# Hybrid attention block: other slots for the sums of x, part of them reloaded in the last unit, larger transfers, and two column blocks of w_out split early and kept in DRAM

## The chip, the core and the metric

The kernel runs on one core of a Trainium2 chip. The metric is device time in microseconds (us) of one execution; the median of several runs counts. A core has TensorE (PE; PEld is its weight load), VectorE (DVE), ScalarE (ACT), GpSimd (POOL) and SyncE (SP, which here issues nearly all DMAs). Each engine works through its own queue in order.

## The reference

The block takes x (2048 tokens by 1024), normalizes it, projects it with w_in, runs two attention mixers (A: a window of 128; B: three dilated groups), gates each with a SiLU path, projects each branch, merges both with sigmoid gates and adds a last projection to x:

```python
h = rms_norm(x, norm_gain[layer])
proj = h @ w_in[layer]
qa, ka, va, qb, kb, vb, ga, gb, mg = jnp.split(proj, split_idx, axis=-1)
...
br_a = ya @ w_branch_a[layer]
br_b = yb @ w_branch_b[layer]
gates = jax.nn.sigmoid(mg.reshape(bsz, S, N_BRANCHES, D).astype(jnp.float32)
                       + b_merge[layer].astype(jnp.float32)).astype(x.dtype)
merged = gates[:, :, 0] * br_a + gates[:, :, 1] * br_b
x = x + merged @ w_out[layer]
```

## The kernel before

Every large product is made of fp16 pairs: a float32 operand is scaled by a power of two and split into a high and a low half (ACT writes the high half, DVE the low one), and three matmuls (high-high, high-low, low-high) stand for one.

**Order of work.** All instructions are written out by hand in time order. `at(t, f)` puts a step on a heap, and `until(t)` emits what is due between the matmuls. In the main stage t counts pairs of projections, in the tail it counts microseconds that the schedule assumes. The constants at the head (T_..., X_...) are these times. A time only sets the place in each engine's queue; what an engine then does depends on what it waits for.

**Pair loop.** There are 14 units of 8 pairs (one unit: a group of heads of A or B). In a pair TensorE projects two blocks of 128 tokens (L735) into the banks `pj`; ACT and DVE take out q, k and v (v's low half at L767), normalize, and SP turns q and k into `kq` by a DMA transpose (L820). Two or three pairs later come the logits (L905), DVE's bias and maximum (L920), ACT's exponentials, a transpose of the probabilities (`pt`, L943) and the products with v (L954). In the third unit of each head pair the three groups of B are merged (L1118 to L1144, then `YPart`).

**Sums of x.** The gate stage uses a Strassen-like scheme of 7 products instead of 8, in which one factor is a block sum of the normalized x: S1 to S4, with two halves p of 512 tokens and 4 chunks c each. `x_sums` (L1223) makes them inside the pair loop, on DVE and ACT, in the tile `sx` (slots 0 to 3 are float32 scratch, 4 to 6 the two halves of a result), and SP stores them to DRAM (`xsd`). The 128 steps are spread evenly over the stretches of pairs in X_SUM.

**Gate stage.** After pair 111 come 12 merge-gate and gate projections, then six groups of 14 products (`gate_group`, L1563; each product has 12 matmuls). `xs_load` (L1490) first brings the sums back: S2 into the tiles `Y00` and `Y01` of pool `y0`, S3 and S1 into slots 2 and 3 of `wt` (with leftovers in `sx` slots 4 to 6), S4 into a free part of XH and XL. T_X holds their times. The products use S2, S3, S1 and S4 in that order in the first group. Beside this `prep` brings each next group's weights: SP loads them (`w_load`, L195), POOL multiplies by the gains (L200), ACT squares (L247), a small matmul sums over partitions (L219), DVE makes the scale, ACT and DVE split (L272, L282); `w_sums` (L1530, L1533) makes the sums of the weights. The small matmul stands in TensorE's queue at a fixed place.

**w_out.** Its four column blocks j are loaded by `b_load` (L1425, four transfers of 256 KB) and split by `b_blocks` (L1415, L1416: seven blocks with three in-place subtractions and one more at L1437) into slot j of `wt`, which the last stage reads. Before, j = 0, 1 and 2 were split in the gate stage (at 68, 103 and 204), using `sx` slots 0 to 3 as raw tile; j = 3 in the branch stage (66), using the tile `wraw`.

**Branch and output stage.** 32 steps of 5.2 us multiply the branch results Y by the branch weights (L359); DVE multiplies each result by its gate (L1708), POOL adds the two (L1715), and `a_blocks` splits the merged blocks (`mm`, L1415 and L1416) and stores them (`mtd`, L1661). PSUM has 8 banks for these results, so TensorE can be at most 8 results ahead of DVE. SP loads the gates three steps ahead (L1698), and near the end of the stage the first merged groups (`M<-mtd`, L1692). The output stage then runs 8 groups of 7 products with `wt` (L1774).

Of the kernel before, what the change touches and what calls it, by code (L numbers as in the profile page):

```python
# [100 lines left out]
X_END = (68.1, 71.1, 75.1)  # L101
X_TH = 1.2
X_SC = (0.25, 0.25, 0.25, 0.0625)
X_SUM = ((5, 16), (19, 33), (44, 59), (68, 83), (93, 104)), 0.2
T_Y = (2.0, 0.8, 1.6, 1.5, 4.0, 26.0, 0.5, 1.3, 2.1, 1.6, 2.0)
T_P = ((0, 0.0, 0.03), (1, 7.0, 31.0), (2, 37.5, 60.5), (3, 69.4, 92.4), (4, 105.8, 128.8), (5, 142.2, 165.2))
T_O = ((0, 60.0, 68.0), (1, 95.0, 103.0), (2, 196.0, 204.0))
T_OB = (58.0, 66.0)
T_G = (173.0, 183.0, 193.0, 194.5)
T_R = (60.0, 1.2)  # L110
T_X = ((1, 0.0), (2, 2.0), (0, 14.0), (3, 22.0))
T_S = (2.0, 11.0, 0.85, 1.6, 0.75, 1.5, 0.9, 1.3, 0.8)
T_H = (176.0, 2.0, 0.02)
T_GATE = (0.1, 0.1, 0.9, 1.0, 1.0)
# [16 lines left out]
def block_kernel(tc, x, w_units, w_gate, w_mrg, w_brn, w_out, w_bra, gain, qkg, sink, bias_a, bias_b, b_merge, out):  # L131
# [54 lines left out]
    def raw_tile():  # L186
        return wp.tile([128, NCH, 384], F32, name="wraw", bufs=1)
# [262 lines left out]
    def at(t, f, *args):  # L450
        seq[0] += 1
        heapq.heappush(heap, (t, seq[0], f, args))
# [796 lines left out]
    def spread(n, parts):  # L1249
# [8 lines left out]
                d -= b - a  # L1258
        return out

    times = spread(128, X_SUM[0])
    for k in range(8):
        x_sums(times[16 * k:16 * k + 16], k // 4, k % 4)
# [2 lines left out]
    t = 0  # L1266
# [102 lines left out]
    def tail_scales():  # L1369

        def tt(*a):
            V.tensor_tensor(*(v[:] for v in a[:-1]), a[-1])

        V.tensor_scalar(so4[:], so[:], 0.25, None, OP.mult)
        for k, (s, inv) in enumerate(((sa, ia), (sb, ib))):
            mi, rm, iv = ucol(), ucol(), ucol()
            for c in range(3):
                tt(mi, mi if c else yi[4 * k], yi[4 * k + c + 1], OP.max)
                yield
            V.reciprocal(rm[:], mi[:])  # L1380
            yield
            tt(rm, rm, s, OP.mult)
            tt(iv, mi, inv, OP.mult)
            yield
            for c in range(4 * k, 4 * k + 4):
                tt(rho[c], rm, yi[c], OP.mult)
            invb.append(iv)
        tt(bnd, invb[0], invb[1], OP.add)
        tt(inv_m, invb[0], invb[1], OP.max)
        yield  # L1390
        V.tensor_scalar(bnd[:], bnd[:], 2.0 ** 31, None, OP.mult)
        V.reciprocal(rmx[:], inv_m[:])
        yield
        s_m, i_m = pow2(bnd[:], "m")
        for c in range(8):
            V.tensor_scalar(rho[c][:], rho[c][:], invb[c // 4][:], rmx[:], OP.mult, OP.mult)
        V.tensor_scalar(inv_m[:], inv_m[:], s_m[:], 0.125, OP.mult, OP.mult)
        V.tensor_scalar(i_o[:], i_m[:], io[:], 16.0, OP.mult, OP.mult)
# [10 lines left out]
    A11, A12, A22, S1, S2, S3, S4 = range(7)  # L1409
    B11, B21, B22, T1, T2, T3, N4 = range(7)  # L1410
    mtd = [dr.tile([4, 128, 7, 4, 2, 128], F16, name=f"mtd{k}") for k in range(2)]
    bw, ms = {}, {}

    def split(hi, lo, v, scale):
# [1 line left out]
                lambda: V.scalar_tensor_tensor(lo, v, scale[:], hi, OP.mult, OP.subtract))  # L1416

    def b_load(j):
        if j < 3:
            rv = sx[:, :4].rearrange("p a b c -> p a (b c)").bitcast(F32)  # L1420
        else:
            rv = raw_tile()[:].rearrange("p a b -> p (a b)")[:, :2048].rearrange("p (a b) -> p a b", b=512)
        for i in range(2):
            for h in range(2):
                nc.sync.dma_start(out=rv[:, 2 * i + h, :], in_=w_out[h, :, 4 * i + j, :])  # L1425
        bw["out", j] = rv

    def b_blocks(t0, j):

        b11, b12, b21, b22 = (bw["out", j][:, k, :] for k in range(4))  # L1430
        sub = {0: (b11, b12, b11), 1: (b12, b22, b12), 3: (b22, b22, b11), 5: (b21, b21, b22)}
        for i, (b, v) in enumerate(((B11, b11), (B22, b22), (B21, b21), (T1, b11), (T3, b12), (T2, b22), (N4, b21))):
            hi, lo = split(wt[0][:, b, j, :], wt[1][:, b, j, :], v, so4)
            at(t0 + T_B[2] * i, hi)
            at(t0 + T_B[2] * i + T_B[3], lambda lo=lo, b=b: (lo(), done.add(("b", j, b))))
            if i in sub:
                at(t0 + T_B[2] * i + T_B[3] + .05, lambda o=sub[i]: V.tensor_tensor(*o, OP.subtract))  # L1437


    def br_load(i):  # L1440
# [39 lines left out]
    def xsum(p, i, c):  # L1480
        m = 4 * p + c
        if i == 1:
            return [s2[p][:, k, c, :] for k in range(2)]
        if i == 3:
            return [X[:, c, 1024 + 512 * p:1536 + 512 * p] for X in (XH, XL)]
        if i == 2 and m > 5 or i == 0 and m > 6:
# [2 lines left out]

    def xs_load(p, i):  # L1490
        assert all(("xs", p, i, c) in done for c in range(4))
        if i == 1:
            for k in range(2):
                nc.sync.dma_start(out=s2[p][:, k], in_=xsd[p][:, i, :, k])
            return
        for c in range(4):
            for k, v in enumerate(xsum(p, i, c)):
                nc.sync.dma_start(out=v, in_=xsd[p][:, i, c, k])

    def xblock(b, c, p):  # L1500
        if b in sidx:
# [101 lines left out]
            yield  # L1603

    t = t0 = clock[0]
    s2 = [y0.tile([128, 2, 4, 512], F16, name=f"Y0{p}") for p in range(2)]
    for i, d in T_X:
        for p in range(2):
            at(t + d + .01 * p, xs_load, p, i)
    at(t + T_R[0], run, tail_scales())  # L1610
    for n, b, d in T_P:
        w_sums(t + d, n)
# [114 lines left out]
    y_part(t + T_Y[4], 2, 6, T_Y[4] - .01, 4)  # L1727
    br_prep(t + T_BR[3], 1)
    br_prep(t + T_BR[4], 2)
    at(t + T_OB[0], b_load, 3)  # L1730
    at(t + T_OB[1], b_blocks, t + T_OB[1], 3)
    y_part(t + T_Y[5], 1, 5)
    left = {}
    for k, (i, q) in enumerate(steps):
# [172 lines left out]
```

## Time and profile before

| | us |
|---|---|
| median of 3 runs | 1914.48 (1914.24 to 1918.62) |
| the profiled execution | 1916.64 |
| its span, first to last instruction | 1914.8 |
| TensorE busy in it | 1887.6 |
| DVE / ACT / POOL busy | 1388.3 / 1157.5 / 760.3 |

The profiler's page gives busy times, groups of instructions by source line, and who waited for whom. The other views used are windows (busy time of each engine between two moments, with the clock that TensorE was granted), waits, the chain that ended last, and timelines; times in them count from the start of the span. In names such as `wt<-xsd` the tile written stands ahead of the arrow. SPq is SP's queue; a row there is the issue of a DMA, not its transfer.

### The profile page before, as it was taken

Reading aid. Unit: us, or ns where it says so; the run is one execution under the profiler, and the core shown is the slowest. Engines: PE = TensorE matmul, PEld = TensorE weight load, DVE = VectorE, ACT = ScalarE, POOL = GpSimd, SP = SyncE. Lnnn points to the kernel's source line nnn. Section 1 sums busy time; section 2 is a strip of 40 time slices with the busy share of each in tenths; the row PEclk is TensorE's granted clock in tenths of the full one; section 3 lists DMA queues with packets and bytes.
Section 4 is the critical chain, followed back from the end, with each engine's and each line's share of the span. In section 5 each row is a group of like instructions: output and inputs, shape, how many; then the busy total and the mean of one; then the engine's idle time right before and its main releaser. Section 6 shows DMA issues by size and latency. Waiting matters only on the chain. (4 is left out here: it accounts for less than half of the span.)

```text
span 1914.8 us, 39519 instructions
## 1 busy us (share of the span) xinstructions
PE 1887.6 (99%) x13493; PEld 1183.4 (62%) x13493; DVE 1388.3 (73%) x3691; ACT 1157.5 (60%) x2692; POOL 760.3 (40%) x1782
## 2 busy tenths in 40 slices
PE   8999999999999999999999999999999999999999
PEld 6566766677766687666876668765434444444444
DVE  7579887898887877878878788777347447876412
ACT  8468776787676776767767677665245444432100
POOL 2224343333456545555545654555011101222543
PEclk9999999999999999999999999999999999999999
DMA  8559988897978878787887878669463345878763
GB/s 290 123 100 177 217 168 166 151 204 167 196 153 180 162 156 168 148 185 159 170 164 143 185 142 163 140 120 197 149 198 105 105 158 182 243 235 258 251 242 146
DMA packets 638601, 333.34 MB, mean 174 GB/s; under 512 B 494272, under 2 KB 572480, under 8 KB 637120
## 3 DMA queue, kind: packets, MB, share of 16 engines
q1 hardware_dynamic: 619968, 322.17, 71.5%
q10 hardware_dynamic: 18432, 8.66, 1.8%
q8 instruction: 105, 1.72, 0.4%
q14 instruction: 96, 0.79, 0.1%
HBM read 138.30 MB, written 73.66 MB: 111 GB/s over the span
## 5 line engine op out<-in xcount | busy, mean ns | idle before, releaser
L735 PE MATMUL pj<-wh,XH 128*128 128x384 f16 x1792 | 585.0, 326 | 4.5 <-DVE vt L767 3.8
L735 PE MATMUL pj<-wh,XL 128*128 128x384 f16 x1792 | 586.8, 327 | 0.0
L735 PE MATMUL pj<-wl,XH 128*128 128x384 f16 x1792 | 585.4, 327 | 0.0
L735 PEld LDWEIGHTS <-XH 128*128 128x128 f16 x3584 | 411.4, 116 | 156.2 <-issue 7.6
L920 DVE CUSTOM_DVE_ANT_0 pr<-s,b,ubuf 128x256 f32<-128x256 f32 (+3 forms) x512 | 218.5, 463 | 44.1 <-PE s L905 42.8
L735 PEld LDWEIGHTS <-XL 128*128 128x128 f16 x1792 | 207.7, 116 | 67.8 <-issue 0.5
L937 DVE SCALAR_TENSOR_TENSOR p<-pr,p 128x512 f16<-128x512 f32 (+2 forms) x256 | 188.4, 736 | 15.2 <-ACT p L933 13.6
L812 POOL COPY spl<-spl 128x256 f16<-128x256 f16 (+1 forms) x224 | 88.6, 425 | 226.3 <-DVE spl L807 223.9
L933 ACT ACTIVATE p<-pr 128x512 f16<-128x512 f32 (+2 forms) x256 | 159.1, 622 | 6.6 <-POOL rs_t L318 0.4
L752 ACT ACTIVATE rw<-pj 128x256 f32<-128x256 f32 (+1 forms) x224 | 86.0, 384 | 109.9 <-PE pj L735 102.6
L905 PE MATMUL s<-kq 128*128 128x256 f16 (+3 forms) x1168 | 147.8, 254 | 3.4 <-DMA kq<-spl 3.4
L954 PEld LDWEIGHTS <-pt 128*128 128x128 f16 x3024 | 125.4, 97 | 33.9
L797 POOL TENSOR_TENSOR rw<-rw,g 128x256 f32<-128x256 f32 (+1 forms) x112 | 89.5, 799 | 124.2 <-DVE rw L791 84.8
L954 PE MATMUL pv<-vt,pt 128*128 128x65 f16 (+1 forms) x3024 | 132.7, 192 | 0.0
L905 PEld LDWEIGHTS <-kq 128*128 128x128 f16 x1184 | 101.6, 98 | 44.9 <-DMA kq<-spl 4.7
L310 POOL TENSOR_TENSOR rs_t<-rs_y 128x8 f32<-128x8 f32 (+1 forms) x112 | 42.0, 375 | 215.7 <-DVE rs_y L302 176.2
L1715 POOL TENSOR_TENSOR kp<-kp,fg 128x512 f32<-128x512 f32 x32 | 45.3, 1419 | 203.5 <-DVE fg L1708 123.1
L791 DVE TENSOR_TENSOR rw<-rw,qr 128x512 f32<-128x512 f32 (+1 forms) x112 | 87.0, 777 | 45.9 <-POOL qr L319 45.3
L928 ACT ACTIVATE pr<-pr,z 128x128 f32<-128x128 f32 (+2 forms) x256 | 98.8, 438 | 35.3 <-DVE z L920 35.1
L359 PE MATMUL fps<-Y,wh 128*128 128x512 f16 x384 | 114.5, 379 | 4.7 <-DVE kp L1708 2.4
L1774 PEld LDWEIGHTS <-M 128*128 128x128 f16 x684 | 66.9, 98 | 78.4
L359 PEld LDWEIGHTS <-wh 128*128 128x128 f16 x640 | 62.2, 98 | 78.0 <-issue 4.3
(289 smaller groups left out, 3900.8 us busy)
## 6 DMA issues: line engine op xcount, KB each, us to landing
wraw<-in_w_units_dram SPq DMA_DIRECT2D x56, 384.0 KB, 4.4
mtd<-mm SPq DMA_DIRECT2D x56, 256.0 KB, 3.8
M<-mtd SPq DMA_DIRECT2D x8, 1792.0 KB, 9.5
zd<-z ACTq DMA_DIRECT2D x128, 66.0 KB, 2.6
zz<-zd SPq DMA_DIRECT2D x64, 132.0 KB, 2.8
xt<-in_x_dram SPq DMA_DIRECT2D x16, 512.0 KB, 8.8
gtd<-yo SPq DMA_DIRECT2D x32, 256.0 KB, 2.9
yo<-gtd SPq DMA_DIRECT2D x32, 256.0 KB, 3.8
```

Of the source, the lines that this page charges most:

```text
L359: out.append(lambda w=w, xx=xx, ch=ch, i=i: T.matmul(ps[:], lhsT=w[:, ch, c0:c0 + 128], rhs=xx[:, ch, ts], start=(i == 0), stop=(i == n - 1)))
L735: out.append(lambda lhs=lhs, rhs=rhs, ch=ch, k=k: T.matmul(ps[:, :384], lhsT=lhs[:, ch, :], rhs=rhs[:, ch, :], start=(k == 0), stop=(k == ...
L752: A.activation(self.rw[:, n * i:n * i + n], self.ps[i][:, :n], AF.Copy)
L791: V.tensor_tensor(q, q, self.rr[:, :n].unsqueeze(2).to_broadcast([128, n, HD]), OP.mult)
L797: G.tensor_tensor(k, k, GT[un.br][:].unsqueeze(1).unsqueeze(1).to_broadcast([128, 2, un.nk, HD]), OP.mult)
L812: G.tensor_copy(sp[:, i, nh:, :, :], sp[:, i, nq:nh, ::-1, :])
L905: T.matmul(self.sv[j][:, o:o + k1 - k0], lhsT=q[:, h, qo:qo + 128], rhs=kt[:, un.nq + kh + v * un.nk, k0:k1], start=(v == 0), stop=(v == 1))
L920: V.tensor_tensor_reduce(out=self.pv[:, j, self.p0:self.p0 + W], in0=self.sv[j], in1=un.bias[:, self.h0 + j, self.b0:self.b0 + W], scale=I ...
L928: A.activation(v, v, AF.Exp, bias=self.stat(j), scale=-1.0)
L933: A.activation(self.sp[:, :128 * n], self.pr, AF.Copy, scale=PSC)
L937: V.scalar_tensor_tensor(self.sp[:, 128 * n:], self.pr, PSC, self.sp[:, :128 * n], OP.mult, OP.subtract)
L954: T.matmul(self.po[:, j, :w], lhsT=p[:, n * j + s, :], rhs=un.v[key][:, vh, c0:c0 + w], start=(k == 0 and s == 0), stop=(k == 2 and s == n ...
```

## The change

It has four parts.

- X_SUM: the stretches of pairs that hold the steps of the sums start and end elsewhere, and each store comes 0.35 instead of 0.2 pairs behind its last step.
- `xs_early`: at pair time 109.0, in the last unit, three DMAs bring S2 of half 0 (4 chunks), S3 of half 1 (chunks 2 and 3) and S1 of half 1 (chunk 3) back into `sx`. S2 of half 0 is then read from `sx` for the whole gate stage.
- `xs_load`: the rest comes in 14 transfers (for each of the two fp16 halves one of up to 4 chunks) instead of 52; the rows stay 1 KB long. S1 starts at 0.06 and 4.0 instead of 14.0, S4 at 14.0 and 15.0 instead of 22.0.
- w_out: the raw tile `rawb` takes the place of one S2 tile. Blocks 2 and 3 are split first, at 48 and 80, into slots 0 and 1 of `wt`, and stored to a DRAM tile `wod`; blocks 0 and 1 follow at 116 and 152 in the same slots. In the branch stage `b_back` loads blocks 2 and 3 into slots 2 and 3, at 40 and 50. The scale `so4` is made at 20 instead of 60.

```diff
-X_SUM = ((5, 16), (19, 33), (44, 59), (68, 83), (93, 104)), 0.2
+X_SUM = ((3, 14.5), (19, 33), (48, 60.5), (71.5, 84.5), (97, 108)), 0.35, 109.0
...
-T_O = ((0, 60.0, 68.0), (1, 95.0, 103.0), (2, 196.0, 204.0))
-T_OB = (58.0, 66.0)
+T_O = ((2, 38.0, 48.0), (3, 68.0, 80.0), (0, 104.0, 116.0), (1, 140.0, 152.0))
+T_OB = ((2, 40.0), (3, 50.0))
...
-T_X = ((1, 0.0), (2, 2.0), (0, 14.0), (3, 22.0))
+T_X = ((1, 1, 0.0), (2, 0, 0.02), (2, 1, 0.04), (0, 0, 0.06), (0, 1, 4.0), (3, 0, 14.0), (3, 1, 15.0))
...
+    def xs_early():
+        for o, p, i, c, n in ((0, 0, 1, 0, 4), (4, 1, 2, 2, 2), (6, 1, 0, 3, 1)):
+            assert all(("xs", p, i, c + k) in done for k in range(n))
+            nc.sync.dma_start(out=sx[:, o:o + n], in_=xsd[p][:, i, c:c + n])
+
+    at(X_SUM[2], xs_early)
...
-        V.tensor_scalar(so4[:], so[:], 0.25, None, OP.mult)
...
+    wod = [dr.tile([128, 2, 7, 512], F16, name=f"wod{k}") for k in range(2)]
...
-        if j < 3:
-            rv = sx[:, :4].rearrange("p a b c -> p a (b c)").bitcast(F32)
-        else:
-            rv = raw_tile()[:].rearrange("p a b -> p (a b)")[:, :2048].rearrange("p (a b) -> p a b", b=512)
+        rv = rawb[:]
...
-            hi, lo = split(wt[0][:, b, j, :], wt[1][:, b, j, :], v, so4)
+            hi, lo = split(wt[0][:, b, j % 2, :], wt[1][:, b, j % 2, :], v, so4)
...
+        if j > 1:
+            for k in range(2):
+                at(t0 + T_B[2] * 6 + T_B[3] + 2 + .1 * k, lambda k=k: nc.sync.dma_start(out=wod[j - 2][:, k], in_=wt[k][:, :, j - 2, :]))
+
+    def b_back(j):
+        for k in range(2):
+            nc.sync.dma_start(out=wt[k][:, :, j, :], in_=wod[j - 2][:, k])
...
-            return [s2[p][:, k, c, :] for k in range(2)]
+            return [sx[:, c, k, :] if p == 0 else s2[:, k, c, :] for k in range(2)]
...
-        if i == 1:
-            for k in range(2):
-                nc.sync.dma_start(out=s2[p][:, k], in_=xsd[p][:, i, :, k])
-            return
-        for c in range(4):
-            for k, v in enumerate(xsum(p, i, c)):
-                nc.sync.dma_start(out=v, in_=xsd[p][:, i, c, k])
+        n = 4 if p == 0 or i == 3 else 2 if i == 2 else 3
+        for k in range(2):
+            if i == 1:
+                v = s2[:, k]
+            elif i == 3:
+                v = (XH, XL)[k][:, :4, 1024 + 512 * p:1536 + 512 * p]
+            else:
+                v = wt[k][:, 4 * p:4 * p + n, 2 if i else 3, :]
+            nc.sync.dma_start(out=v, in_=xsd[p][:, i, :n if i != 1 else 4, k])
...
-    s2 = [y0.tile([128, 2, 4, 512], F16, name=f"Y0{p}") for p in range(2)]
-    for i, d in T_X:
-        for p in range(2):
-            at(t + d + .01 * p, xs_load, p, i)
+    rawb = y0.tile([128, 4, 512], F32, name="Y00")
+    s2 = y0.tile([128, 2, 4, 512], F16, name="Y01")
+    for i, p, d in T_X:
+        at(t + d, xs_load, p, i)
+    at(t + 20, lambda: V.tensor_scalar(so4[:], so[:], 0.25, None, OP.mult))
...
-    at(t + T_OB[0], b_load, 3)
-    at(t + T_OB[1], b_blocks, t + T_OB[1], 3)
+    for j, d in T_OB:
+        at(t + d, b_back, j)
```

## The prediction, made blind

> **What bounds the kernel now.** I read the page first: TensorE is busy for nearly the whole span.
>
> ```profile
> PE 1887.6 (99%) x13493; PEld 1183.4 (62%) x13493; DVE 1388.3 (73%) x3691; ACT 1157.5 (60%) x2692; POOL 760.3 (40%) x1782
> ```
>
> Of the 1914.8 us span 27.2 us are without a matmul, and the change removes no matmul. So it can win only these idle spells and what TensorE loses at a lower granted clock behind them. Second came TensorE's waits (total, times, longest):
>
> ```profile
> PE fps L1563 <- DMA wt<-xsd: 4.6, 1, 4.6
> PE pj L735 <- DVE vt L767: 3.8, 6, 1.6
> PE s L905 <- DMA kq<-spl: 3.4, 3, 2.5
> PE fps L359 <- DVE kp L1708: 2.4, 3, 1.8
> PE fps L359 <- DVE fg L1708: 1.4, 2, 1.0
> PE fps L219 <- ACT wl L247: 1.0, 1, 1.0
> PE fps L359 <- DVE Y L1353: 0.9, 2, 0.5
> ```
>
> That is 17.5 us. Third, the timeline of TensorE, for where they lie (the bracket is the idle time before the row and what ended it):
>
> ```profile
> 661.18 0.32 PE L735 MATMUL pj<-wh,XH 128*128 128x384 f16 x1 [0.74 <-DVE vt L767]
> 667.32 0.61 PE L905 MATMUL s<-kq 128*128 128x256 f16 x4 [2.52 <-DMA kq<-spl]
> 1393.64 1.01 PE L1563 MATMUL fps<-wt,wh 128*128 128x512 f16 x2 [4.62 <-DMA wt<-xsd]
> 1690.79 0.59 PE L359 MATMUL fps<-Y,wh 128*128 128x512 f16 x2 [1.79 <-DVE kp L1708]
> ```
>
> Three places, and the change touches each: the slots of the x sums in the pair loop (661 and 667), the head of the gate stage (1394), and the branch stage beside the last split of w_out (1691; the fg wait of 1.0 comes soon after it).
>
> **Part 1: the slots of the sums.** The windows below are pairs of the loop, from the first L735 matmul of one to that of the next (48 a pair): 46 to 49, then 71 and 95. The columns are length, busy time of PE, PEld, DVE, ACT and POOL, granted clock, DMA share, GB/s.
>
> ```profile
> 646.40:655.70 9.30, 9.30 (x82) 6.88 (x81) 7.74 (x23) 6.16 (x15) 3.31 (x12) 1.00 0.91 185
> 655.70:669.30 13.60, 10.34 (x82) 6.93 (x81) 11.10 (x29) 9.53 (x21) 5.44 (x15) 0.95 1.18 217
> 669.30:679.60 10.30, 10.30 (x82) 8.38 (x81) 7.36 (x26) 6.48 (x16) 4.13 (x14) 0.91 0.77 183
> 679.60:689.00 9.40, 9.40 (x83) 8.31 (x82) 6.81 (x21) 6.41 (x18) 4.79 (x14) 1.00 0.86 168
> 900.90:911.50 10.60, 9.71 (x83) 6.86 (x81) 7.73 (x24) 8.46 (x19) 4.73 (x14) 1.00 1.11 226
> 1142.10:1153.10 11.00, 9.43 (x82) 6.87 (x80) 6.83 (x22) 6.43 (x15) 4.73 (x14) 1.00 0.74 165
> ```
>
> Pairs 47 and 48 take 23.9 us where 46 and 49 take 18.7: 5.2 us lost, 3.3 idle and the rest at the clock of 0.95 and 0.91. Pairs 71 and 95 lose about 1.2 and 1.6 against 9.4. All three come two or three pairs after a stretch of sums opens (44, 68, 93), while the merges of the unit before still run on DVE. From 622.6 to the second wait, DVE's groups of the sums are:
>
> ```profile
> L459 DVE TENSOR_TENSOR sx<-sx 128x512 f32<-128x512 f32 x3 | 2.6, 860 | 0.0
> L1229 DVE TENSOR_TENSOR sx<-XH,XL 128x512 f32<-128x512 f16 x2 | 1.4, 685 | 0.0
> L1235 DVE SCALAR_TENSOR_TENSOR sx<-sx 128x512 f16<-128x512 f32 x1 | 1.2, 1221 | 0.0
> ```
>
> So 5.2 us of DVE stand ahead of a wait of 3.3. The new stretches open at 48, 71.5 and 97, where these pairs are over. The bounds are 0 (the merges alone are late enough) and 8.0; I take 6.5, near the upper one because the 5.2 us exceed the wait, and leave 1.5 for new collisions, since 62 pair lengths now hold the 128 steps that 66 held, and pairs 59, 83 and 104 to 107 get some.
>
> New in this stage is the reload at 109.0: three DMAs, 1792 KB together, on SP just ahead of pair 107's kq transposes; behind them in SP's order stand those, two zz loads and a pt transpose. SP's rows and the logits that need the first kq block:
>
> ```profile
> 1271.01 2.55 SPq L820 DMA_TRANSPOSE kq<-spl  x2
> 1277.66 0.60 PE L905 MATMUL s<-kq 128*128 128x256 f16 x4
> M<-mtd SPq DMA_DIRECT2D x8, 1792.0 KB, 9.5
> DMA to landing us min/median/max: 2.8/2.8/2.8
> ```
>
> The last row is that of the two transposes: they land at 1273.8, 3.9 us ahead of need. M<-mtd, of the reload's size, lands after 9.5 us. If the transposes queue behind as much, the first lands near 1280.5, a wait of 2.8, and pair 48 shows 0.9 (its length) to 1.6 (the clocks of both rows) more at half clock after such a wait: 4.4 at most, 0 if they pass. At the 361 GB/s of a row below, 1792 KB take 5.1 us, so about a us is late: I take 1.0. (DMA: Bandwidth & Descriptors in the Trainium skill, section on queues, rings and completion order, says that each DMA engine starts a ring's descriptors in order, so a bulk load stands ahead of later transposes. By that rule it is 1 to 4.4, not 0. No row quoted here shows it for transposes.) Part 1: 5.5 us won.
>
> **Part 2: the head of the gate stage.** The first row is the whole first group (14 products of 12 matmuls), the next two tell the DMA rate, the fourth is TensorE behind its wait.
>
> ```profile
> 1368.10:1411.50 43.40, 38.77 (x171) 17.03 (x170) 17.78 (x33) 17.28 (x29) 4.07 (x4) 0.92 0.83 261
> 1376.00:1378.00 2.00, 2.00 (x11) 0.88 (x10) 0.75 (x1) 0.88 (x2) 0.00 (x0) 1.00 1.10 361
> 1382.00:1384.00 2.00, 2.00 (x11) 0.93 (x10) 0.13 (x1) 0.00 (x0) 0.00 (x0) 1.00 0.64 190
> 1394.00:1398.00 4.00, 4.00 (x12) 1.51 (x11) 0.30 (x3) 0.42 (x2) 0.00 (x0) 0.50 0.86 276
> ```
>
> Then SP's queue, two products of the output stage without a wait (24 matmuls), and the weight chain of the second group: POOL's gains and the sum on TensorE that needs ACT's squares of them.
>
> ```profile
> 1369.60 2.10 SPq L1494 DMA_DIRECT2D Y<-xsd  x4
> 1371.92 10.24 SPq L1498 DMA_DIRECT2D wt<-xsd  x12
> 1384.32 1.92 SPq L195 DMA_DIRECT2D wraw<-in_w_mrg_dram  x4
> 1387.27 9.14 SPq L1498 DMA_DIRECT2D wt<-xsd  x14
> 1779.23 5.18 PE pj L1774 x24
> 1390.63 3.03 POOL L200 TENSOR_TENSOR wraw<-wraw,gn 128x512 f32<-128x512 f32 x3 [1.78 <-DMA wraw<-in_w_mrg_dram]
> 1397.43 0.21 PE L219 MATMUL fps<-wsq,ones 128*128 128x4 bf16 x1
> ```
>
> At 5.18 us for two products the group needs 36.3 us and takes 43.4: 7.1 lost, 4.6 in the wait for S1 and 2.5 at the clock of 0.50. S1 is wanted at the ninth product, 1368.1 + 8 x 2.59 = 1388.8, but SP issues its first load at 1387.27, behind S2 and S3, of which S3 went out in 128 KB pieces, and behind a weight load. While the 512 KB loads drain the rate is 361 GB/s, among the pieces 190.
>
> After the change, S2 of the first half and part of S3 and S1 are in place; ahead of S1's first half stand 1024 + 1024 + 512 KB, then its own 1024: 3.67 MB, at 361 GB/s 10.2 us behind the first data (some 2 us behind the first issue, 1371.5), about 1384 with the landing, near 5 us early. Ten issues at 0.53 (2.10 for 4) hold SP for 5.3 us. What is late next is the weight chain of the second group: S1's second half (768 KB) and the weights (1024 KB) make 5.5 MB, 15.2 us, so the last quarter lands near 1388.3. POOL's gains (1.01 each, in a row behind the first quarter) end near 1390.5, ACT's last square soon after. TensorE, 7 us earlier than now, comes to the L219 sum after 9 matmuls of the ninth product, at 1390.8: a wait of a us or less, I take 0.8. At the group's mean 261 GB/s the weights land near 1394, the wait is about 5 and half clock adds up to 2.5: the bad bound is 7.5, the good one 0. (TensorE: Matmul & The Clock Gate in the Trainium skill, section on why this matters for your kernels, allows TensorE idle gaps up to some 3 us. The row of 2.52 us at 667 with pair 48's 0.91 speaks against it; by the rule a 2 us wait would cost 2, here up to 3.6.) Part 2: 6.3 won.
>
> **Part 3: the splits of w_out.** Block 3 is now split in the branch stage. DVE's groups there from 1667 to 1692, then its share in the gate stage, then its last gate sum:
>
> ```profile
> L1416 DVE SCALAR_TENSOR_TENSOR wt<-wraw,ubuf,wt 128x512 f16<-128x512 f32 x7 | 5.2, 743 | 0.2 <-ACT wt L1415 0.2
> L1437 DVE TENSOR_TENSOR wraw<-wraw 128x512 f32<-128x512 f32 x4 | 3.8, 952 | 0.0
> 1500.00:1550.00 50.00, 50.00 (x235) 22.63 (x233) 25.86 (x49) 21.12 (x35) 4.03 (x4) 1.00 0.23 79
> 1598.35 0.68 DVE L1583 TENSOR_TENSOR fc<-fps,fc 128x512 f32<-128x512 f32 x1
> ```
>
> TensorE runs ahead of DVE's L1708 by at most 8 banks, 20.7 us; the waits of 1.79 and 1.0 say that DVE is this late. Taking 9.0 us from it removes the 1.79 and the 1.0 (2.8). Block 2's split no longer shares the gate stage's tail, where fc is summed as late as 1598; the branch stage's first loads, queued behind its store, start by my estimate some 3 us earlier (four block splits of 0.74 stood between its last sums), and the 0.9 on Y goes. In the gate stage DVE is half idle, ACT more, so the extra round fits. The L219 wait of 1.0 came as ACT's squares stood behind a split; of the new times (48, 80, 116, 152) that at 80 starts behind the squares: 0.7 won, bounds 0 and 1.0. The stores to DRAM (two of 896 KB a block) meet 79 GB/s there: nothing. Reading back, 2 x 1792 KB at 40 and 50 of the branch stage, goes ahead of gate loads and mm stores: free at best, 5.1 us of lateness twice at worst, of which banks absorb all but some 2.5; I take 0.3. so4's move is one small DVE operation. Part 3: 2.8 + 0.9 + 0.7 - 0.3 = 4.1.
>
> **Sum.** 5.5 + 6.3 + 4.1 = 15.9 us. The profiled execution took 1916.6 (1914.8 and 1.8 around it), so 1900.7; it stands 2.2 above the median, so the median becomes 1898.6. With every upper bound (8.0, 7.1, 2.8 + 0.9 + 1.0) it is 1894.7.
>
> **Rivals.** (a) The merges, not the sums, make the loop's waits: Part 1 gives 6.5 less and costs 1.0; 9.4 won, 1905.1. Against it, DVE spends 5.2 us on sums ahead of a 3.3 us wait; for it, only pairs with sums are seen at this place. (b) The DMA, not SP, is the limit: 261 GB/s holds with large transfers, the weights come late (7.5) and the reload and the reading back cost 4.4 and 2.5: 6.5 + 7.1 + 4.4 - 14.4 = 3.6 won, 1910.9. Against it speaks the 361. (c) Slower: the splits inside the gate stage put ACT behind late w_out loads, with the squares queued behind, and TensorE waits at L219 in each of four groups. Today's one case costs 1.0. With 2 us at half clock behind each wait (pair 48's 1.6, the 2.5 at 1394), it decides from 2 us of wait in each group, 16 in all, which is the whole gain; at 3.5, 22 in all, the time is 1920.6. Against it: DVE half idle, loads issued 10 us or more ahead. (d) The reload isn't early: should SP reach it only behind the last main-stage store, 5.1 us of transfer return ahead of the weights, the wait there is 5.9 with 2.5 at half clock: 7.6 less, 8.3 won, 1906.2. Against it, its sums end two pairs before.
>
> **Chances.** The forecast 0.64, (a) 0.14, (b) 0.07, (c) 0.07, (d) 0.05, no gain at all 0.03. A measurement of this kernel tells about 0.3%, 5.7 us: faster is below 1908.7. The forecast, (a), (d) and a little of (b) are faster, 0.84; the rest of (b) and no gain 0.09; (c) 0.07. The range reaches from 1893, a little below all upper bounds for small waits not counted here, to 1908, past (a) and (d); outside are (b), (c) and no gain, 0.17.
>
> **What would show it.** Right: no wait on vt or kq near pairs 47, 71 and 95, the first gate group in 36 to 38 us at clock 1.00, a wait under 1.5 at its L219, no L1708 wait near 1690. Wrong: a kq wait just behind the reload, an L219 wait above 3, new vt waits at pairs 59, 83 or 107, or L1708 waits that begin where blocks 2 and 3 are read back.

## The result and the profile after

The changed kernel takes 1903.01 us (median of 4 runs, 1900.73 to 1903.83) beside 1915.45 of the kernel before in the same set: 12.4 us less at the medians, ratio 0.9931 with a 95% interval of 0.9913 to 0.9948. A second set gave 1901.29 beside 1913.93, ratio 0.9934 (0.9920 to 0.9947). The prediction said 1898.6, 15.9 us less. Three executions far longer than all others of their kernel (2173 us of the kernel before, 2817 and 5131 us of e6) are left out of the ratios. The profiled execution took 1902.5 us, span 1900.7.

This is the busy line of the profile's page after. TensorE has the same number of matmuls, and 18.7 us of the span are without one, instead of 27.2.

```profile
PE 1882.0 (99%) x13493; PEld 1182.4 (62%) x13493; DVE 1379.7 (73%) x3691; ACT 1157.6 (61%) x2692; POOL 762.6 (40%) x1782
```

These are some of TensorE's waits after (total, times, longest). The 4.6 us for S1 and the L1708 waits are gone; a kq wait and an L219 wait of 1.8 us each are there.

```profile
PE pj L735 <- DVE vt L767: 3.3, 5, 0.8
PE fps L219 <- ACT wl L247: 2.2, 2, 1.8
PE s L905 <- DMA kq<-spl: 1.8, 1, 1.8
```

The timeline shows where: the kq wait at the very place of before's 2.52, a vt wait in pair 64 that before did not have, SP's issue of the second gate group's weights (at 1384.32 before), POOL's gains of them, and TensorE's sum that needs these.

```profile
667.20 0.61 PE L905 MATMUL s<-kq 128*128 128x256 f16 x4 [1.78 <-DMA kq<-spl]
818.15 0.32 PE L735 MATMUL pj<-wh,XH 128*128 128x384 f16 x1 [0.85 <-DVE vt L767]
...
1376.50 4.60 SPq L195 DMA_DIRECT2D wraw<-in_w_mrg_dram  x4
...
1385.77 4.03 POOL L200 TENSOR_TENSOR wraw<-wraw,gn 128x512 f32<-128x512 f32 x4 [34.80 <-DMA wraw<-in_w_mrg_dram]
...
1390.60 0.17 PE L219 MATMUL fps<-wsq,ones 128*128 128x4 bf16 x1 [1.81 <-ACT wl L247]
```

Two windows follow (length, busy time of PE, PEld, DVE, ACT, POOL, granted clock, DMA share, GB/s): pair 47 with the last 1.5 us of pair 46, then the first gate group. The group has clock 1.00 and is 5.1 us shorter. Pair 47's stretch has clock 1.00 too, and DVE is busy 8.19 us there instead of 11.10, yet the DMA share is 1.20, as high as the 1.18 before.

```profile
655.20:668.50 13.30, 11.23 (x94) 8.01 (x93) 8.19 (x26) 9.00 (x20) 5.44 (x15) 1.00 1.20 201
1365.90:1404.20 38.30, 36.49 (x171) 16.44 (x169) 17.72 (x34) 17.23 (x29) 4.03 (x4) 1.00 0.76 248
```

The next table has the stages in the profiled execution of each kernel (us): the loop, from the first L735 matmul of pair 0 to the first gate product, then the first gate group, the other five, the branch stage, and the output stage with what follows it.

```
                     loop   1st group  groups 2-6  branch  output
before              1297.8     43.3      182.8     171.9   148.6
after               1295.7     38.3      181.9     165.8   148.8
e5 after again      1294.2     38.5      181.6     166.5   148.8
e1 slots only       1293.4     42.4      182.9     170.1   148.6
e2 w_out only       1298.1     43.6      181.4     167.7   149.1
e3 no sums          1290.2     38.1      181.5     166.3   149.0
e4 piece moved      1293.9     37.6      181.6     166.9   148.9
e6 small pieces     1295.8     45.2      181.4     167.2   148.6
e7 reload late      1293.5     46.3      181.7     165.8   149.2
e8 both             1295.2     36.3      182.8     165.8   148.9
e9 block 3 late     1294.8     38.3      181.4     167.3   148.9
e10 back twice      1294.2     37.9      182.9     187.5   148.8
e11 best slots      1292.4     36.3      181.8     166.0   148.8
e12 block 2 late    1294.9     42.1      181.6     170.5   148.6
```

The loop of one and the same code varies by 2 to 3 us between executions (old slots: before, e2, e12; new slots: after, e1, e5, e6, e7, e9, e10), so below it is compared by means over these. The branch stage varies too: before and e1 have the same code there and differ by 1.8 us.

### The profile page after: what moved, and what is told of

Same layout as the page of the kernel before. It is cut to its first block, busy times and chain, and to the rows that moved or that the text cites. A ratio compares the mean times of both kernels' runs of the same rounds, so it can differ in the third digit from the quotient of the medians.

```text
span 1900.7 us, 39497 instructions
## 1 busy us (share of the span) xinstructions
PE 1882.0 (99%) x13493; PEld 1182.4 (62%) x13493; DVE 1379.7 (73%) x3691; ACT 1157.6 (61%) x2692; POOL 762.6 (40%) x1782
## 4 chain that ended last, share of the span: by engine, by line
PE 74%; DVE 9%; DMA 6%; ACT 4%; issue 3%; POOL 3%; SPq 1%; DVEq 0%; ACTq 0%; POOLq 0%
PE pj L735 38%; PE pj L359 11%; PE fps L359 6%; PE s L905 5%; PE fps L1787 5%; PE pv L954 4%; PE fps L1575 2%; PE pj L1787 2%; DMA wraw<-in_w_mrg_dram 1%; PE pj L1575 1%; DMA kq<-spl 1%; PE pj L635 1%; DVE wl L279 1%; DMA mtd<-mm 1%; DVE pr L920 1%
## 5 line engine op out<-in xcount | busy, mean ns | idle before, releaser
L735 PE MATMUL pj<-wh,XH 128*128 128x384 f16 x1792 | 584.6, 326 | 4.0 <-DVE vt L767 3.3
L735 PE MATMUL pj<-wh,XL 128*128 128x384 f16 x1792 | 586.2, 327 | 0.0
L735 PE MATMUL pj<-wl,XH 128*128 128x384 f16 x1792 | 584.8, 326 | 0.0
L735 PEld LDWEIGHTS <-XH 128*128 128x128 f16 x3584 | 411.2, 116 | 154.3 <-issue 5.7
L735 PEld LDWEIGHTS <-XL 128*128 128x128 f16 x1792 | 207.6, 116 | 67.4
L1787 PE MATMUL fps<-wt,M 128*128 128x512 f16 (+1 forms) x516 | 110.3, 374 | 0.3 <-DVE pr L1802 0.3
```

Source lines behind the costliest of these rows:

```text
L735: out.append(lambda lhs=lhs, rhs=rhs, ch=ch, k=k: T.matmul(ps[:, :384], lhsT=lhs[:, ch, :], rhs=rhs[:, ch, :], start=(k == 0), stop=(k == ...
L1787: mm.append(lambda ch=ch, k=k, w=w, i=i: T.matmul(ps[:, :cols.stop - cols.start], lhsT=m[:, a, ch, k, :], rhs=wt[w][:, b, ch, cols], start ...
```

## The experiments

The theory at the start is the prediction's: the sums of x make DVE late two or three pairs after their stretches open, order and size of the loads make the head of the gate stage slow, and block 3 of w_out makes DVE late in the branch stage. Rivals: transfers and merges make the loop's waits; the reload alone, or the order alone, did the gate head; block 2's tail, not block 3, did the branch stage.

**e1, the slots alone.**

```diff
-X_SUM = ((5, 16), (19, 33), (44, 59), (68, 83), (93, 104)), 0.2
+X_SUM = ((3, 14.5), (19, 33), (48, 60.5), (71.5, 84.5), (97, 108)), 0.35
```

> The kernel before with nothing changed but the five stretches of the sums and the delay of their stores. Theory of the prediction (DVE's sums cause the waits of pairs 47, 71 and 95): these waits go, the loop from pair 0 to the first gate product becomes 6.5 us shorter (bounds 0 and 8.0), and the time falls by as much. Rival (the merges and the transfers of that place cause them, the sums add little): the kq wait at pair 47 stays at 1.5 to 2.5 us, new vt waits of 0.5 to 0.9 appear at other pairs, and the loop gains 1 to 3 us. The gate and branch stages keep their lengths within 1 us in both.

The time is 1910.72 us beside 1913.26, ratio 0.9988 (0.9979 to 0.9996): 2.3 us won by the ratio, 0.8 to 4.0, not 6.5. That is the rival's 1 to 3 us, though the kq wait is smaller than its 1.5 to 2.5. On TensorE's timeline a kq wait of 1 us is still in pair 47, and pairs 64 and 88 have vt waits that they did not have:

```profile
665.75 0.61 PE L905 MATMUL s<-kq 128*128 128x256 f16 x4 [0.97 <-DMA kq<-spl]
...
816.72 0.33 PE L735 MATMUL pj<-wh,XH 128*128 128x384 f16 x1 [0.87 <-DVE vt L767]
...
1057.26 0.32 PE L735 MATMUL pj<-wh,XH 128*128 128x384 f16 x1 [0.62 <-DVE vt L767]
```

**e2, Part 3 alone.** This is the kernel before with T_O, T_OB, the DRAM tiles and so4's place as after; slots 0 to 3 of sx stay the raw tile.

> The kernel before with Part 3 alone: the blocks of w_out split at the new places, blocks 2 and 3 kept in DRAM and read back. The prediction prices this at 4.1 us (2.8 + 0.9 in the branch stage, 0.7 in the gate stage). Rival from the two traces (the branch stage came out without any wait, 165.8 us for 768 matmuls, against 171.9): 6 us in the branch stage and 0.7 in the gate stage, 6.5 to 7 in all, as waits shorter than those listed add up too. If the shorter branch stage came from the earlier start of the changed gate stage instead, less than 4. The loop and the first gate group stay as before.

The time is 1910.29 us beside 1913.26, ratio 0.9982 (0.9973 to 0.9990): 3.4 us won, 1.9 to 5.2. That is nearer the prediction's 4.1 than the rival's 6.5, and it does not exclude the third case, under 4. In the profiles groups 2 to 6 are 1.3 us shorter, and the branch stage is 4.2 shorter than in before and 2.4 shorter than in e1, which has before's code there. The waits of 1.79 and on Y are gone, but the 1.0 on fg stays. All of TensorE's waits in the branch stage (L1708 is L1713 here):

```profile
PE fps L359 <- DVE fg L1713: 1.0, 1, 1.0
PE fps L359 <- DVE kp L1713: 0.2, 1, 0.2
```

**e3, no sums.**

```diff
-            at(ts[k], f, *args)
+            if f is lo:
+                at(ts[k] + X_SUM[1], store, args[1])
...
+    at(X_SUM[0][0][0] - .5, lambda: V.memset(sx[:, 4:7], 0.0))
```

> The changed kernel without the arithmetic of the sums of x: the 12 DVE and 4 ACT steps of each of the 8 chunks are left out, the tiles are zeroed once, the 32 stores, the reload and all that follows stay (so the products with S1 to S4 are of zeros). Theory of the prediction (the sums are what DVE is late by): the kq wait at pair 47 and the vt waits at pairs 59 to 107 go, and the loop becomes 3 us or more shorter than the changed kernel's 1295.7 from pair 0 to the gate stage. Rival (merges and transfers): the kq wait of 1.8 at pair 47 and the vt waits at pairs 64, 88 and 95 (0.6 to 0.9 each) stay, the loop gains under 1.5 us.

There is one run, 1896.83 us; it leaves out the sums and so computes something else. TensorE's waits in the loop, where after has 3.3 on vt and 1.8 on kq:

```profile
PE s L905 <- DMA kq<-spl: 1.0, 2, 0.8
PE pj L735 <- DVE vt L767: 0.7, 1, 0.7
```

The vt waits of pairs 64 and 88 are gone, so the sums cause them though they end some four pairs earlier. In the changed kernel DVE's last step of the sums ahead of pair 64 ends at 775.1; from there to the wait at 818 DVE is idle only four times, 0.8 to 1.1 us each, once a pair for POOL. Ahead of pair 88 it is the same. The 0.7 left is pair 95's, and 0.8 of kq is pair 47's: these two places wait without any sums.

The loop of e3 is 1290.2 us. It is a single execution, so the sums over the loop below carry a doubt of 2 to 3 us; single pairs repeat more closely. With e3 as the zero, each pair's loss in the other kernels is (its length, from L735 to L735, less that in e3; us):

```
pair             10     14     47     48     64     71     88     95
old: before     0.0   0.57   3.33   0.96   0.0    1.23   0.0    0.88
     e2         0.0   0.55   2.90   0.84   0.0    1.22   0.0    1.04
     e12        0.0   0.55   1.37   0.0    0.0    0.87   0.0    0.62
new: after      1.32  0.91   1.43   0.0    0.79   0.0    0.57   0.10
     e1         0.73  0.91   0.35   0.0    0.81   0.0    0.58   0.17
     e5         0.0   0.89   0.64   0.0    0.87   0.0    0.65   0.17
     e6         1.05  0.92   0.28   0.0    0.87   0.41   0.66   0.12
     e7         1.23  0.88  -0.12   0.0    0.88   0.0    0.65   0.13
```

The means over the three old and seven new loops are 1297.0 and 1294.5 us, against 1290.2 without sums. (e9 and e10 are not listed; they lie among the other new ones but in pair 95, where they take 0.3 less than e3.) So the sums cost 6.8 in the old slots and 4.3 in the new. The wait of pair 10 ends on a transfer (pt), the others listed there on vt and kq.

**e4, the third branch matrix's 1 MB moved from pairs 46 and 47 to pairs 94 and 95.**

```diff
-        u = 3 + k
+        u = 11 if k == 2 else 3 + k
```

> The changed kernel with the 1 MB piece of the third branch matrix (four loads of 256 KB and two squares on ACT) moved from unit 5, where it is loaded in pairs 46 and 47, to unit 11, pairs 94 and 95, which has none. Theory that the kq wait at pair 47 is a queue of transfers (share of the DMA engines above 1 in pair 47): the kq transposes land in 3 to 4 us instead of 6 to 7, the wait of 1.78 goes, the loop gains 1.5 to 2.5 us, or gives it back at pair 95 if the same queue forms there. Theory that DVE is late there: the wait stays at 1.5 or more and the time is the same.

The kq transposes of pair 47, by SP's instructions on that tile, in the changed kernel and here (number, duration, start; time to landing):

```profile
L820 SPq DMA_TRANSPOSE kq<-spl x2: 1227/1700/2173, 661.0 to 662.4; - x2
...
DMA to landing us min/median/max: 5.5/5.8/6.1
```

```profile
L820 SPq DMA_TRANSPOSE kq<-spl x2: 1240/1584/1927, 659.7 to 661.7; - x2
...
DMA to landing us min/median/max: 3.0/3.2/3.3
```

The wait is gone and pair 47 is 0.98 us shorter even than without sums; pair 95 loses 0.44. So what is left of this wait goes with these transfers (the two squares on ACT that moved with them were not tried apart). In the time it can't be told: 1899.47 beside 1913.26, ratio 0.9931 (0.9919 to 0.9942), the changed kernel's own.

**e5, the changed kernel again.**

> The changed kernel once more, as the control of this set: some 13 us (0.7%) under the kernel before, with the loop 1295 to 1297 us from pair 0 to the gate stage, the first gate group 38.3, the branch stage 165.8 to 166.5, and a mean granted clock of 1.00 in every run where the kernel before has 0.997 to 0.999. Both theories expect the same; it tells how much the stages vary from run to run.

The time, the first group and the branch stage are as expected; the loop, 1294.2, is a little under. Its L219 wait is 2.08 us.

**e6, small pieces.**

```diff
-            nc.sync.dma_start(out=v, in_=xsd[p][:, i, :n if i != 1 else 4, k])
+            for c in range(n if i != 1 else 4):
+                nc.sync.dma_start(out=v[:, c], in_=xsd[p][:, i, c, k])
```

> The changed kernel with the 14 loads of up to 512 KB behind the loop cut again into 46 of 128 KB, in the same order and from the same times; the reload of 1792 KB in the last unit stays. If the order and the reload made the head of the gate stage fast, and the size of the pieces does not matter: first gate group 38 to 39 us, L219 wait near 1.8. If SP's issues and the rate of small pieces matter, as the prediction has it (190 to 276 GB/s, 0.53 us per issue): S1's first half, now behind 20 pieces ahead of it, still lands before 1388.8, but the weights behind it land 5 us or more later, the L219 wait is 5 to 9 us with half clock behind it, and the first group takes 44 to 48 us.

(It makes 50 pieces of the 14 loads, not 46.) The time is 1908.99 us, ratio 0.9974 (0.9964 to 0.9983), 7.7 above e5. SP issues the second group's weights at 1384.54, 8 us later than the 1376.50 of the changed kernel, and TensorE waits 6.42. The 26 pieces of 128 KB in the first row leave SP one each 0.51 us, which is 256 GB/s, at a DMA share of 0.85; so SP's issues most likely set this rate. First SP's queue and then TensorE in this kernel's timeline; S1 itself is not waited for.

```profile
1371.13 13.31 SPq L1511 DMA_DIRECT2D wt<-xsd  x26
1384.54 1.93 SPq L195 DMA_DIRECT2D wraw<-in_w_mrg_dram  x4
...
1395.06 0.16 PE L219 MATMUL fps<-wsq,ones 128*128 128x4 bf16 x1 [6.42 <-ACT wl L247]
```

**e7, the reload at the loop's end.**

```diff
-    at(X_SUM[2], xs_early)
...
+    at(t - .01, xs_early)
```

> The changed kernel with the three DMAs of the reload (1792 KB) issued at the end of the loop ahead of the other loads of the sums, not in the last unit. Prediction's rival (d): 5.1 us of transfer come back ahead of the weights, the L219 wait of the second group's scale is 5 to 7 us, half clock follows, and the time is 5 to 8 us above the changed kernel. If the queue is not what sets the weights' landing, the L219 wait stays near 1.8. The kq wait in pair 107 is 0 in both kernels, so the loop gains nothing from a late reload.

The time is 1907.53 us, ratio 0.9968 (0.9956 to 0.9981), 6.2 above e5: rival (d) took 7.6 for it. TensorE waits 1.2 us for S2 of the second half and 5.38 at L219. Both waits are below, then the windows of the longer one and of what follows it, where the clock is near half again.

```profile
PE fps L1574 <- DMA Y<-xsd: 1.2, 1, 1.2
...
1393.55 0.16 PE L219 MATMUL fps<-wsq,ones 128*128 128x4 bf16 x1 [5.38 <-ACT wl L247]
```

```profile
1388.20:1393.50 5.30, 0.00 (x0) 0.00 (x0) 1.35 (x3) 2.90 (x8) 4.03 (x4) 0.87 1.09 338
1393.50:1399.50 6.00, 5.95 (x17) 2.15 (x17) 3.04 (x9) 3.38 (x5) 0.00 (x0) 0.55 0.56 187
```

The expectation called the early reload free in the loop. It is not quite: the two transposes behind it (issued as pair 109 begins) are just in time or a little late. In the changed kernel's first profile they land in 6.7 and 5.8 us without a wait; e4, e5, e6 and e11 wait 0.5, 0.4, 0.5 and 1.1 us for them. This is e5's row:

```profile
1273.92 0.61 PE L905 MATMUL s<-kq 128*128 128x256 f16 x4 [0.36 <-DMA kq<-spl]
```

**e8, the piece moved, and every group's scale chain 2.2 us later.**

```diff
-T_W = (0.3, 5.5, 1.1, 8.5, 0.9, 15.6, 16.1, 17.0, 0.9, 0.8)
+T_W = (0.3, 5.5, 1.1, 8.5, 0.9, 17.8, 18.3, 19.2, 0.9, 0.8)
```

> The changed kernel with two edits: the third branch matrix's piece in unit 11 (as before in this set of runs), and the scale chain of every gate group's weights, from the sum on TensorE on, 2.2 us later. Theory that TensorE comes to the sum before ACT's squares are through: the L219 wait of 1.8 goes, the first group takes 36.5 us, nothing else becomes late since the next group's weights are split 8 us before they are needed; with the moved piece 3 to 4 us under the changed kernel in all. Rival: the chain behind the sum (scale, 8 splits) is late for the next step (the differences of the blocks), and a new wait at the second group's first products gives it back: same time as with the piece alone.

The L219 wait goes and the first group takes 36.3 us, the time of its matmuls. But the fifth takes 37.7 instead of 36.5 (a wait of 0.94 on the gate sum fd), and the tail of the loop had a kq wait of 1.66 in this execution. The time is 1900.80 us, ratio 0.9935 (0.9923 to 0.9948): no gain that can be told from e5, though 3 to 4 us were expected.

**e9, block 3 split in the branch stage again, block 2 still early.**

```diff
-T_O = ((2, 38.0, 48.0), (3, 68.0, 80.0), (0, 104.0, 116.0), (1, 140.0, 152.0))
-T_OB = ((2, 40.0), (3, 50.0))
+T_O = ((2, 38.0, 48.0), (0, 104.0, 116.0), (1, 140.0, 152.0))
+T_OB = ((2, 40.0),)
+T_O3 = (58.0, 66.0)
...
+    at(t + T_O3[0], b_load, 3)
+    at(t + T_O3[1], b_blocks, t + T_O3[1], 3)
```

> The changed kernel with block 3 of w_out split in the branch stage again (loaded at 58, split from 66, as before); block 2 stays in DRAM from the gate stage on. Theory of the prediction (the 9.0 us of DVE for block 3 are what makes DVE eight banks late there): the L1708 waits of 1.8 and 1.0 return, the branch stage takes 168.5 to 171 us instead of 165.8 to 166.9, 3 us of the time. Rival (the late start behind block 2's tail before, or nothing but the spread of runs, made the difference): the branch stage stays under 167.5, and the time is that of the changed kernel.

The time is 1901.95 us, ratio 0.9937 (0.9921 to 0.9952): the changed kernel's. All of TensorE's waits in the branch stage (lines are one higher in this kernel):

```profile
PE fps L360 <- DVE fg L1722: 0.4, 1, 0.4
PE fps L360 <- DVE kp L1722: 0.4, 2, 0.2
```

DVE has the 9 us of block 3 back at the old place, and the wait of 1.79 does not come back; 0.4 on fg stands where the 1.0 was. So block 3's work alone does not make these waits, as the prediction had it.

**e10, blocks 2 and 3 read back twice.**

```diff
-            nc.sync.dma_start(out=wt[k][:, :, j, :], in_=wod[j - 2][:, k])
+            for _ in range(2):
+                nc.sync.dma_start(out=wt[k][:, :, j, :], in_=wod[j - 2][:, k])
```

> The changed kernel with blocks 2 and 3 each read back twice (4 x 1792 KB in the branch stage instead of 2 x). The prediction prices the reading back at 0.3 us, 0 at best and 2.5 at worst. If the banks absorb it, the second reading costs under 0.5 us and the branch stage stays at 165.8 to 167; if the gate loads and stores queued behind it come late, L1708 or gate waits of 1 us or more appear some 10 us behind 40 and 50 of the stage, and it takes 2 to 5 us more.

The time is 1922.57 us, ratio 1.0038 (1.0025 to 1.0052): 21 us above e5, which neither side had. It does not price the transfer, because the second load of a tile waits on SP for the first to land. SP's own waits at this line, then its queue, in which the gate loads and stores stand behind:

```profile
SPq L1448 <- DMA wt<-wod: 27.5, 4, 7.4
```

```profile
1637.71 16.40 SPq L1448 DMA_DIRECT2D wt<-wod  x4
1654.16 0.69 SPq L1712 DMA_DIRECT2D kp<-mgd  x1
```

TensorE then waited 9.81 and 4.66 us on L1722's gates. The price of one reading back stays open; in the changed kernel no wait of TensorE follows either of the two.

**e11, three edits together.** These are e4's, e8's for the second group alone, and

```diff
-X_SUM = ((3, 14.5), (19, 33), (48, 60.5), (71.5, 84.5), (97, 108)), 0.35, 109.0
+X_SUM = ((5, 8), (19, 35), (48, 59.5), (71.5, 83.5), (97, 108)), 0.35, 109.0
```

> The changed kernel with three edits: the third branch matrix's piece in unit 11, the scale chain 2.2 us later for the second gate group alone, and the sums of x in five stretches (5 to 8, 19 to 35, 48 to 59.5, 71.5 to 83.5, 97 to 108), which end one pair earlier ahead of the waits seen in pairs 64 and 88 and leave out pairs 10 and 14. Theory that sums left in DVE's queue cause these four waits (0.87, 0.91, 0.84 and 0.62 us more than without sums): most of the 3.2 us go, with 1.5 of pair 47 and 2 of the gate group 5 us or more under the changed kernel. Rival: 2.4 steps per pair instead of 2.06 make DVE late in other pairs, and no more than 3 us are won.

The time is 1897.61 us beside 1914.01, ratio 0.9914 (0.9901 to 0.9927). This is the fastest kernel of the study that computes the block. It is 3.7 us under e5 at the medians, with intervals that overlap a little, and lies between the 5 of the theory and the 3 of the rival. Pairs 10, 14 and 88 lose nothing now and pair 64 0.49, but pair 30 loses 1.09 (inside the denser stretch 19 to 35) and pair 109 1.12 behind the reload. The loop is 2.2 us over e3, half of the 4.3.

**e12, block 2 in the gate stage's tail again, block 3 early.** The kernel before with

```diff
-T_O = ((0, 60.0, 68.0), (1, 95.0, 103.0), (2, 196.0, 204.0))
-T_OB = (58.0, 66.0)
+T_O = ((3, 68.0, 80.0), (0, 104.0, 116.0), (1, 140.0, 152.0), (2, 196.0, 204.0))
+T_OB = ((3, 50.0),)
```

> The kernel before with block 3 alone split early and kept in DRAM; block 2 is split at 204 of the gate stage, in its tail, as before, and blocks 0 and 1 at the new times. The run without block 3's early place (branch stage 167.3 us, no L1708 wait over 0.4) left block 2's tail as the cause. By that theory the branch stage here keeps the waits of 1 to 1.8 us of the kernel before and takes 169.5 to 172 us, though 9.0 us of DVE have left it, and the time is that of the kernel before less the 1 us of the gate stage. By the theory of the prediction (block 3's DVE work) the waits go and it takes 167 to 168 us, as in the kernel with both blocks early (167.8). If either block alone is enough for DVE to come in time, both this and the run before it lie near 167.5.

The time is 1912.77 us beside 1912.97, ratio 1.0000 (0.9991 to 1.0009): no gain. The waits expected from block 2's tail are not the ones that came. All of TensorE's waits in the branch stage:

```profile
PE fps L359 <- DVE Y L1353: 1.2, 3, 0.5
PE fps L359 <- ACT Y L1350: 1.1, 1, 1.1
```

The wait of 1.79 is gone here as in e2, where block 3 is also away. The 1.0 on fg is gone too, but e2 has it still, and so has the changed kernel in e6 (0.95). The Y waits grow from 0.9 to 2.3 us, and TensorE falls to half clock behind them (windows of the waits, of what follows, and after it):

```profile
1606.00:1612.40 6.40, 4.15 (x18) 1.55 (x16) 4.71 (x8) 2.10 (x3) 1.70 (x1) 1.00 1.01 368
1612.40:1616.00 3.60, 3.60 (x10) 1.31 (x9) 0.33 (x1) 0.58 (x2) 1.26 (x1) 0.53 0.99 364
1616.00:1620.00 4.00, 4.00 (x20) 1.84 (x19) 3.94 (x8) 3.57 (x8) 0.00 (x0) 1.00 0.33 126
```

The branch stage then compares as follows (us). Block 2's place is worth some 3 to 4 us, block 3's 1 or less:

```
                          block 3 in branch stage   block 3 early
block 2 in gate tail      171.9, 170.1              170.5
block 2 early             167.3                     165.8 to 167.2, 167.7 (e2)
```

## Why the prediction was right or wrong

The direction and the range were right; the gain forecast was 3 us too good. Part by part, by the means of the profiled executions with the same code in the stage:

```
                               forecast    measured
Part 1, slots and reload          5.5      2.4  (loop, 1297.0 to 1294.5)
Part 2, head of the gate stage    6.3      4.6  (first group, 42.8 to 38.2)
Part 3, gate stage, L219          0.7      1.1  (groups 2 to 6, 182.8 to 181.7)
Part 3, branch stage              3.4      4.7  (171.0 to 166.3)
sum                              15.9     12.8  (12.4 and 12.6 at the medians)
```

(Means: old first group before, e1, e2, e12, new after, e5, e9, e10; groups 2 to 6 before and e1 against e2, e12, after, e5, e6, e7, e9, e10; branch before and e1 against after, e5, e6, e7.)

That the sum came so near is partly luck: Parts 1 and 2 won 4.8 us less than forecast, and Part 3 won 1.7 more, mostly for another reason than its largest term had. Of the four signs of being right only one held in full, that no L1708 wait is near 1690. The waits at pairs 47 and 95 are still there, the first group took 38.3 us where 36 to 38 were said, at the clock of 1.00, and the L219 wait is above 1.5. Of the signs of being wrong only one came, and in other executions of the changed kernel: a kq wait behind the reload.

**Part 1: the step "I take 6.5" failed, in two ways.** First, its upper bound of 8.0 held 4.3 us lost in pairs 47 and 48, as one execution showed them; e12, with the same slots, loses 1.4 there. And "the 5.2 us exceed the wait" did not make DVE the only cause: these 5.2 us are spread over 44.7, and the row quoted for that pair had a DMA share of 1.18. Pair 47 loses 2.5 us on the mean with the old slots, 0.5 with the new, and -1.0 with the 1 MB of the piece elsewhere too (e4), where the transposes land in 3.2 us: 2.0 go with the slots, 1.5 with the queue of transfers. How much of the 2.0 is DVE's arithmetic is not shown, for with the old slots a store of the sums also goes out just ahead of these transposes. This is before's row, and the transposes follow at 660.42:

```profile
659.69 0.43 SPq L1239 DMA_DIRECT2D xsd<-sx  x1
```

So rival (a), merges and not sums, can be right for pair 95's last 0.7 and no more, and what it left out were the transfers. On the mean pairs 47, 48, 71 and 95 won 4.5.

Second, the 1.5 left for new collisions was too little and at the wrong pairs. They came in pairs 10, 14, 64 and 88, some 2.7 us on the mean, not at 59, 83 or 104 to 107. In pairs 64 and 88 DVE has not yet worked off what the stretch before them left: it is idle there only for POOL, and in e11, whose stretches end one pair earlier, pair 88 loses nothing and pair 64 0.49. The forecast looked for collisions inside a stretch; the backlog is paid at the next place where TensorE needs DVE at once.

**The reload** was priced at 1.0 and costs 0 to 1.1, by the rows of pair 109. DMA: Bandwidth & Descriptors in the Trainium skill, section on queues, rings and completion order, says that on each DMA engine descriptors are taken in ring order. The trace agrees: behind the reload the two kq transposes land in 6.7 and 5.8 us, without it in 2.8. These are the DMA issues of the changed kernel around the reload, with KB and the median us to landing (the third kq transpose comes 9 us later and takes 3.1):

```profile
sx<-xsd SPq DMA_DIRECT2D x1, 1024.0 KB, 5.1
sx<-xsd SPq DMA_DIRECT2D x1, 512.0 KB, 6.2
...
kq<-spl SPq DMA_TRANSPOSE x3, 5.8
```

The 3.9 us by which they landed ahead of need in the kernel before covered this nearly whole.

**Part 2: mechanism right, two sizes off.** S1 is in place and is not waited for, and the clock is 1.00. Large transfers and reload are both needed: without the one the group is 7.0 us longer (e6), without the other 8.0 (e7), and with either missing it is longer than before's 42.8. What is late is then the weights, not S1, by the L219 waits of 6.4 and 5.4 (in e7 S2 too, by 1.2). The L219 wait was mis-sized, 0.8 against 1.8 and 2.1. Counted from the group's first product, TensorE was forecast at the sum after 22.7 us and came after 22.8. But the gains were forecast to end after 22.4, and they end after 23.8 (1389.80), with ACT's last square at 1390.55: the first quarter of the weights lands only at 1385.6, 19.6 us into the group. The estimate was 361 GB/s without a break; by their landing times in the trace the loads behind the first took 15.7 us for 4.98 MB, some 318 GB/s. And the 7.1 lost before are 6.5 on the mean of four executions.

**Part 3: the sum about right, its main cause wrong.** The step "taking 9.0 us from it removes the 1.79 and the 1.0" gave the gain to block 3. e12 takes these 9 us away and the branch stage is no more than 0.5 us under the mean before, because the Y waits behind block 2's tail take the place of the others; e9 puts them back, and the stage takes 167.3 beside 165.8 to 167.2. What counts is that block 2's split has left the gate stage's tail. The traces show how, counted from the branch stage's first matmul (us):

```
                                     before   e12    e2    e9   after
block 2 split in the tail              yes    yes    no    no    no
DVE's last gate sum (fc) starts        4.1    4.2   0.2   0.2   0.2
SP issues the stage's first gate load  6.2    6.3   2.2   2.2   2.2
the first yg (for Y) has landed       13.1   13.9  10.0   8.8   9.6
TensorE waits on Y                     0.9    2.3    0     0     0
```

Behind the splits DVE makes the last gate sum 4 us later, its store goes out as much later, and the stage's first loads stand behind this store in SP's queue. ACT's split of Y waits for yg. The prediction had this very step, with "some 3 us earlier", but gave it only the smaller term (0.9). It fits the 1.79 too: DVE's split of block 3 just ahead of the place of this wait starts 92.6 us into the stage in e9, and 96.7 and 96.1 in before and e1. So by this reading the eight banks cover DVE's lag, even with block 3, as long as the stage's loads come in time.

The 1.0 on fg was put down to block 3 as well, but it stays in e2 and e6 without that block. In e2, as before, DVE is idle for 1.4 us ahead of it until POOL has added two results, and then splits merged blocks first. Why it is 1.0 in some executions and 0.4 or nothing in others is open.

The stage won 4.7 and not 3.4; after has no wait at all there. The 0.7 for L219 was near, 1.1 by the mean, 1.0 by its wait. For the 0.3 of the reading back no run shows a price.

**Rivals (b) and (c)** did not come: with large transfers and the early reload the L219 wait was at most 2.1 us, and of the later groups none waited more than 1.3 us there (one, in e10).

## What to carry to other kernels

A wait that ends on a transfer is first compared with that transfer's own issue and landing, and with the DMA share of the window, before a busy engine nearby is called its cause. When work is moved to a gap, look for its price not in the gap but at the next point where the critical engine needs that engine at once; a run with the work left out shows how much any placing of it can win at most. And a loss behind a wait that is near to dropping the clock is to be priced from several executions, not one.

## What the runs showed of the hardware

TensorE's clock halved after idle time that was spread out, too. In e12 four waits of 0.32, 1.07, 0.41 and 0.45 us within 4.0 us were followed by 3.4 us at half speed (clock 0.53 over the 3.6 us of the window above, so 0.47 x 3.6 / 0.5), while single waits of 1.81 (after) and 2.08 us (e5) at L219 left the clock at 1.00. Before's 0.74 and 2.52 within 7 us brought it down, e2's 0.76 and 1.95 did too (0.91 in pair 48), e12's 0.73 and 1.29 at the same place did not. TensorE: Matmul & The Clock Gate in the Trainium skill, section on what is actually happening, tells of a window of about 3.4 us that runs freely; the length of e12's slow spell agrees with it. The Trainium skill's advice on that page, section on why this matters for your kernels, of no gaps over some 3 us does not cover these cases: none of the gaps named here reached it.

Two loads of the same tile in a row (e10) cost the branch stage 21 us: the DMA that waited for an earlier one to land held everything behind it on SP, here for 16.4 us.

In e6 SP issued pieces of 128 KB one each 0.51 us, which is 256 GB/s, while loads of 512 KB reached 361 GB/s in the kernel before.
